# Weight sums made in memory around changes of operand, and a residual in row halves, in a split-fp32 decoder block

## The chip, the cores and the metric

One core of a Trainium2 chip runs one launch of the kernel. The metric is the device time in microseconds (us); a second execution is recorded by the hardware profiler. The core's engines work side by side, each in the order in which its instructions stand: TensorE (PE) multiplies, VectorE (DVE) and ScalarE (ACT) work on tiles, GpSimd (POOL) and SyncE (SP) here mostly issue DMAs. A DMA that an engine issues waits in that engine's order for what it needs, and everything behind it waits too.

## The reference

A decoder block in fp32 with 512 rows and width 2048. Two token mixers share one input projection, and the rest is a GeGLU channel mixer; the part that the change touches is the second half:

```
h    = rmsnorm(x) * g                     # x: 512 x 2048, after the mixers' residual
up   = h @ ffn_w_up                       # 2048 x 12288
up   = causal_dwconv(up, width 3)
gate, val = split(up)                     # 6144 columns each
x    = x + (gelu(gate) * val) @ ffn_w_down  # 6144 x 2048
out  = rmsnorm(x) * final_g
```

## The kernel before

**Precision.** Every fp32 operand is split in two: `h`, a rounded copy in fp32r (cast, ACT, L115), and `l`, the operand less `h` (DVE, L116). A product is three matmuls (`h·h`, `h·l`, `l·h`).

**Stages.** Input projection and mixers, the output projection (to about 561 us), the up product (to about 1575), the down product (to about 2052), and a tail with the last two pairs of rows of the down weights and the final norm.

**Products.** Up and down product use Strassen and Winograd's scheme: an operand tile of 2 x 2 quarters needs four sums of quarters, and seven block products take the place of eight. A tile is `q`, eight slots of 128 x 256: the quarters stand in slots 4 to 7, the four sums go to slots 0 to 3, and slots 0 to 6 are then split into a pair `wh`, `wl` (weights) or `ah`, `al` (activations). One **unit** is the seven products of one weight tile with one activation tile, 42 matmuls with 256 columns (`product`, L790), which add to seven PSUM banks. A **block** is the units that add to the same banks: 24 blocks of eight in the up product (gate and value by turns, two blocks to a group), and in the down product three chunks of 8, 8 and 6 activation tiles, each with four blocks, one to a column block of the output. At the end of an up block `combine` (L813) makes four quarters of the seven banks, and a convolution, a GELU and the multiplication follow as steps that are spread over the next block (`later`, L804); the results go to memory as `ad` (POOL, L869). At the end of a down block the banks are added to a residual tile `xs`, which POOL loads (L905) and writes back (L941).

**Weight sums.** For most weight tiles VectorE makes the sums: L590 (two of them at once, 128 x 512), L591 and L592. For 96 units, the last up block and all of the down product, L590's two sums are made beforehand in memory: POOL issues a copy and an accumulating DMA of 256 KB each (`make`, L681), one DMA to each up unit, and the load then takes the two sums (L584) and three quarters (L585).

**Order.** Weights and activations stand in one list, `stream`, each with `load`, `sums` and `pair`. `prepare` (L655) keeps the loads two places ahead of the pair, and the sums one. `ready(u)` says how far it must be before unit `u`'s products: two units' weights ahead, with the activations listed behind them. There are three `q` slots (pool `wq`), three pairs of weights, and one tile for each activation, which is free for the next chunk once its last product is through. An activation of the down product is listed after unit `s - 8 + spread[i] + 3`, where `s` is the chunk's first unit (L721 to L727). A **change of operand** is the stretch around `s` in which all activation tiles are replaced, one after the other; there are three (1: from up to down product, 2 and 3: between chunks). From the up product on each engine's order is as written in the program.

**The opening of the up product.** The first up block's activations come from the residual rows: four transposes (PE, L706) and an evacuation (ACT, L708) for each of two halves, sums (DVE, L615 to L617), and a pair. They are prepared one unit ahead of their product, beside that unit's weights. The residual rows are scaled first (`scale_rows`, on DVE at L696 and on ACT at L698).

Of the kernel before, what the change touches and what calls it, by code (L numbers as in the profile page):

```python
# [65 lines left out]

@with_exitstack
def hybrid_block(ctx: ExitStack, tc: tile.TileContext, x, xT, w_in, w_out, w_up, w_dn, w_us, w_ds, w_dl, wab, wsT, vec, bs, vgb, fg, out):
# [476 lines left out]

    x2[0] = load_x(0)
# [22 lines left out]

    def slots(name, n=8):  # L570
        return wq.tile([P, n, 256], F32, name=name, tag=name)

    class Weights:
# [5 lines left out]
        def load(self):  # L579
            self.q = q = slots("q")  # L580
            if self.made is None:
                nc.sync.dma_start(q[:, 4:8], self.src)
            else:
                nc.sync.dma_start(q[:, 2:4], self.made)  # L584
                nc.sync.dma_start(q[:, 4:7], self.src[:, 0:3])  # L585

        def sums(self):
            q = self.q
            if self.made is None:
                nc.vector.tensor_tensor(q[:, 2:4], q[:, 5:7], q[:, 7:8].broadcast_to([P, 2, 256]), ALU.add)  # L590
            nc.vector.tensor_tensor(q[:, 1], q[:, 2], q[:, 6], ALU.add)  # L591
            nc.vector.tensor_tensor(q[:, 0], q[:, 1], q[:, 4], ALU.add)  # L592
# [7 lines left out]
    class Acts:  # L600
# [18 lines left out]
        def pair(self):  # L619
# [3 lines left out]
            if self.fill is not None and self.m in (1, 3):  # L623
                scale_rows(2 + self.m // 2)
# [52 lines left out]
    sums_src = [w_us[m] for m in range(8)] + [w_ds[n, p] for c in CHUNKS for n in range(4) for p in c]  # L677
    for k, src in enumerate(sums_src):
        made[n_up - 8 + k] = tc.dram_tile([32, 2048], F32, name=f"made{k}")

    def make(u):  # L681

        k = u // 2
        if k < len(sums_src):
            how = {"accum_op": ALU.add, "max_dma_last_dim": 8192} if u % 2 else {"max_dma_last_dim": 8192}
            nc.gpsimd.dma_start(made[n_up - 8 + k], sums_src[k][u % 2], **how)  # L686
# [34 lines left out]
    spread = (0, 2, 3, 5, 7, 9, 10, 12)  # L721
# [16 lines left out]
    for u, (src, _) in enumerate(units):  # L738
        place[u] = len(stream)
        stream.append(Weights(src, made[u].rearrange("(p b) (c d e) -> (p b c) d e", p=32, c=4, d=2) if u in made else None))  # L740
# [34 lines left out]

    first = a_place[0]
# [7 lines left out]
    done[:] = [first + 2, first + 1, first + 1]  # L784
# [43 lines left out]
    def up_block(g, val, u0):  # L828
        q = {}
        for m in range(8):  # L830
# [5 lines left out]
            make(u0 + m)  # L836
# [56 lines left out]
    def down_block(ci, n, u0):  # L893
# [3 lines left out]
        for m in range(size):  # L897
            prepare(ready(u0 + m))
            if m == (6 if u0 == n_up else 1):
# [4 lines left out]
                xs[n] = pools["x"].tile([P, NS, 512], F32, name="xs", tag="xs", bufs=2)  # L904
                nc.gpsimd.dma_start(xs[n], x2d[n])  # L905
# [4 lines left out]
        X = xs[n]  # L910
        X11, X12, X21, X22 = X[:, 0:2, 0:256], X[:, 0:2, 256:512], X[:, 2:4, 0:256], X[:, 2:4, 256:512]
        c1, c6, c5, c7 = (pools["x"].tile([P, 2, 256], F32, name="cc", tag="cc", bufs=4) for _ in range(4))
        nc.scalar.copy(c1, q[1])  # L913
        tt(X11, X11, q[2], ALU.add)
        nc.scalar.copy(c6, q[6])
        nc.scalar.copy(c5, q[5])
# [4 lines left out]
            lambda: tt(X11, X11, c1, ALU.add),  # L921
            lambda: tt(c6, c6, c1, ALU.subtract),
# [14 lines left out]
        for i in range(4):  # L937
            later(at + i, steps[2 * i])
            later(at + i, steps[2 * i + 1])
        if ci < 2 or n < 2:  # L940
            later(at + 3, lambda: nc.gpsimd.dma_start(x2d[n], X))  # L941
# [6 lines left out]
    for n in range(2):  # L948
        xs[n] = slots("q").rearrange("p a b -> p (a b)").rearrange("p (a b) -> p a b", a=NS)
        nc.sync.dma_start(xs[n], x2d[n])  # L950
# [6 lines left out]
    for st in range(NS):  # L957
# [4 lines left out]
        for n, (i, d, lo, hi) in enumerate(pieces):  # L962
# [6 lines left out]
            t = xs[d][:, st, lo:hi]  # L969
            nc.vector.tensor_tensor(t, t, ps, ALU.add)  # L970
            sq = pools["x"].tile([P, 512], F32, name="sq", tag="cc", bufs=4)
# [16 lines left out]
        for n in order:  # L988
            _, d, lo, hi = pieces[n]
            t = xs[d][:, st, lo:hi]  # L990
# [70 lines left out]
```

## Time and profile before

| | us |
|---|---|
| median of three runs | 2107.61 (2106.12 to 2108.34) |
| profiled execution | 2107.67 |
| span of its instructions | 2106.0 |
| PE busy | 2048.9 (97%) |
| VectorE busy | 1746.8 (83%) |
| ScalarE busy | 911.5 (43%) |
| POOL busy | 185.9 (9%) |

The profiled execution's own time is the span and 1.67 us around it. The rows of slices show the span in 40 equal parts of 52.65 us, each digit the busy share in tenths. A row of windows has the length, then busy time and number of instructions of each engine, the granted clock of TensorE as a share of full speed, the mean busy share of the DMA engines, and GB/s. A row of groups has line, engine, operation, what is written from what, the shapes, the count, then busy us and mean ns of one, then idle time ahead of it and what ended most of it. A row of waits reads: engine and what waited, what it waited for, us in total, times, longest. Rows of DMA issues have KB each and the median us from issue to landing. Matmuls overlap, so PE's busy time counts no less than a stretch in which matmuls follow each other without a gap; a few matmul records are missing.

### The profile page before, as it was taken

How to read it: one execution, taken by the hardware profiler on the slowest of the kernel's cores; microseconds unless marked ns; L12 is line 12 of the kernel's file. 1: busy time of each engine (PE TensorE's matmuls, PEld its weight loads, DVE VectorE, ACT ScalarE, POOL GpSimd, SP SyncE). 2: the span in 40 equal slices, each digit the busy share in tenths (PEclk: the TensorE clock that was granted, in tenths of full speed). 3: DMA queues.
4: the chain of work that ended last, by engine and by line, in shares of the span. 5: the costliest groups of instructions: out<-in, count | busy, mean ns of one | idle time of the engine just before them, and what ended most of it. 6: DMA issues, size and time to landing. Idle time of an engine off the chain costs nothing.

```text
span 2106.0 us, 34882 instructions
## 1 busy us (share of the span) xinstructions
PE 2048.9 (97%) x14488; PEld 1928.0 (92%) x14488; DVE 1746.8 (83%) x2249; ACT 911.5 (43%) x899; POOL 185.9 (9%) x310
## 2 busy tenths in 40 slices
PE   9999999999889999999999999999988998999998
PEld 7888888888679999999999999999988998999996
DVE  7588972735379999999999999999989788778876
ACT  6445322413264444444444444444454344444443
POOL 1000000000010111111111112112110000000001
PEclk9999999999899999999999999999998999999999
DMA  8222322434133656556557557557565555645663
GB/s 276 89 84 95 102 100 100 160 104 166 70 103 118 175 152 185 163 161 188 155 166 195 161 156 200 152 156 198 164 190 175 206 177 193 233 163 202 231 235 120
DMA packets 91647, 338.08 MB, mean 161 GB/s; under 512 B 12768, under 2 KB 13408, under 8 KB 75616
## 3 DMA queue, kind: packets, MB, share of 16 engines
q1 hardware_dynamic: 71712, 236.60, 33.9%
q0 software_dynamic: 19200, 98.58, 17.0%
q8 instruction: 113, 1.85, 0.4%
q10 hardware_dynamic: 576, 0.66, 0.1%
q14 instruction: 46, 0.38, 0.1%
HBM read 304.34 MB, written 81.79 MB: 183 GB/s over the span
## 4 chain that ended last, share of the span: by engine, by line
PE 84%; DVE 10%; DMA 4%; issue 1%; ACT 1%; SPq 0%; DVEq 0%; ACTq 0%
PE qs L800 56%; PE ps L153 9%; PE ps L152 9%; PE ps L151 9%; DVE wl L116 3%; DVE al L116 2%; DMA q<-ad 1%; DMA q<-w_dn 1%; DMA q<-w_up 1%; DVE q L591 1%; DVE q L615 1%; PE qs L152 1%; PE qs L153 1%; PE qs L151 1%; DVE q L592 0%
## 5 line engine op out<-in xcount | busy, mean ns | idle before, releaser
L800 PE MATMUL qs<-al,wh 128*128 128x256 f32 x2688 | 763.8, 284 | 3.6 <-DVE al L116 3.5
L800 PE MATMUL qs<-ah,wh 128*128 128x256 f32 x2688 | 764.4, 284 | 2.7 <-DVE pad L817 1.8
L800 PE MATMUL qs<-ah,wl 128*128 128x256 f32 x2688 | 763.4, 284 | 2.8 <-DVE wl L116 2.8
L115 ACT CAST wh<-q 128x1792 fp32r<-128x1792 f32 (+1 forms) x282 | 476.7, 1691 | 651.1 <-PE qs L800 474.6
L116 DVE TENSOR_TENSOR wl<-q,wh 128x1792 fp32r<-128x1792 f32 (+1 forms) x282 | 567.9, 2014 | 55.4 <-ACT wh L115 55.1
L800 PEld LDWEIGHTS qs<-al,wh 128*128 128x128 f32 x2688 | 518.8, 193 | 4.5 <-DVE al L116 4.5
L800 PEld LDWEIGHTS qs<-ah,wh 128*128 128x128 f32 x2688 | 518.8, 193 | 3.2 <-DVE pad L817 2.0
L800 PEld LDWEIGHTS qs<-ah,wl 128*128 128x128 f32 x2688 | 518.7, 193 | 3.2 <-DVE wl L116 3.2
L800 PE MATMUL qs<-wh,ah 128*128 128x256 f32 x1232 | 353.7, 287 | 11.0 <-ACT cc L913 4.5
L800 PE MATMUL qs<-wl,ah 128*128 128x256 f32 x1232 | 353.7, 287 | 7.4 <-DVE wl L116 7.4
L800 PE MATMUL qs<-wh,al 128*128 128x256 f32 x1232 | 352.9, 286 | 3.9 <-DVE al L116 3.9
L800 PEld LDWEIGHTS qs<-wh,ah 128*128 128x128 f32 x1232 | 240.9, 196 | 12.2 <-ACT cc L913 4.9
L800 PEld LDWEIGHTS qs<-wl,ah 128*128 128x128 f32 x1232 | 240.9, 196 | 9.2 <-DVE wl L116 9.2
L800 PEld LDWEIGHTS qs<-wh,al 128*128 128x128 f32 x1232 | 240.8, 195 | 4.3 <-DVE al L116 4.3
L116 DVE TENSOR_TENSOR wl<-wraw,wh 128x1024 fp32r<-128x1024 f32 (+2 forms) x105 | 118.2, 1126 | 147.6 <-ACT wh L115 147.2
L115 ACT CAST wh<-wraw 128x1024 fp32r<-128x1024 f32 (+2 forms) x105 | 102.2, 975 | 272.2 <-PE ps L152 141.0
L151 PE MATMUL ps<-xgh,wh 128*128 128x512 f32 x384 | 152.5, 398 | 0.1
L152 PE MATMUL ps<-xgl,wh 128*128 128x512 f32 x384 | 152.2, 397 | 0.0
L153 PE MATMUL ps<-xgh,wl 128*128 128x512 f32 x384 | 150.5, 397 | 0.1
L591 DVE TENSOR_TENSOR q<-q 128x256 f32<-128x256 f32 x280 | 118.6, 424 | 29.7 <-DMA q<-w_dn 20.1
L686 POOL DMA_DIRECT2D made<-w_ds x176 | 115.3, 755 | 283.0 <-DMA made<-w_ds 273.8
L590 DVE TENSOR_TENSOR q<-q 128x512 f32<-128x512 f32 x184 | 126.1, 685 | 6.4 <-DMA q<-w_up 6.2
(244 smaller groups left out, 2418.5 us busy)
## 6 DMA issues: line engine op xcount, KB each, us to landing
q<-w_up SPq DMA_DIRECT2D x184, 512.0 KB, 3.6
made<-w_ds POOLq DMA_DIRECT2D x176, 256.0 KB, 4.4
q<-w_dn SPq DMA_DIRECT2D x88, 384.0 KB, 3.3
wraw<-w_in SPq DMA_DIRECT2D x28, 1024.0 KB, 4.8
q<-made SPq DMA_DIRECT2D x96, 256.0 KB, 2.6
wraw<-w_out SPq DMA_DIRECT2D x16, 1024.0 KB, 4.8
ad<-gate POOLq DMA_DIRECT2D x48, 256.0 KB, 2.4
q<-ad SPq DMA_DIRECT2D x24, 512.0 KB, 3.3
```

The lines of the kernel that those rows point to most:

```text
L115: nc.scalar.copy(h, src)
L116: nc.vector.tensor_tensor(l, src, h.bitcast(F32), ALU.subtract)
L151: nc.tensor.matmul(ps, lhsT=ah, rhs=bh, start=start, stop=False)
L152: nc.tensor.matmul(ps, lhsT=ah, rhs=bl, start=False, stop=False)
L153: nc.tensor.matmul(ps, lhsT=al, rhs=bh, start=False, stop=stop)
L590: nc.vector.tensor_tensor(q[:, 2:4], q[:, 5:7], q[:, 7:8].broadcast_to([P, 2, 256]), ALU.add)
L591: nc.vector.tensor_tensor(q[:, 1], q[:, 2], q[:, 6], ALU.add)
L615: nc.vector.tensor_tensor(q[:, 2:4], q[:, 7:8].broadcast_to([P, 2, 256]), q[:, 5:7], ALU.subtract)
L686: nc.gpsimd.dma_start(made[n_up - 8 + k], sums_src[k][u % 2], **how)
L800: nc.tensor.matmul(q[p][:, t], lhsT=x_, rhs=y_, start=first and t == 0 and n == 0, stop=last and t == 1 and n == 2, skip_group_check=True)
```

## The change

1. **Four sums instead of two, and other units.** `made_units` lists 46 units whose four sums are all made in memory: the first up block, and at each chunk the eight units before its first (in the down product only) and as many behind it as the chunk has activations. The last up block keeps two sums in memory. The other 50 down units have none: VectorE makes all four sums. A whole unit takes six DMAs on POOL (two copies and two accumulating ones of 256 KB, an accumulating one of 256 KB and one of 128 KB); the DMAs of neighbouring units are interleaved. The first up block's 48 stand on POOL behind the loads of the residual for the output projection; the other 244 are spread over the first 184 up units. A whole unit's load is 512 KB of sums and 384 KB of quarters.
2. **Activations earlier.** `spread` is (0, 1, 3, 4, 6, 7, 9, 10) instead of (0, 2, 3, 5, 7, 9, 10, 12).
3. **A fourth load buffer.** From the seventh unit of the down product on every fourth `q` comes from another pool.
4. **Residual in row halves.** Two tiles of 512 KB instead of one of 1024 KB, loaded in the second and the fourth unit of a block. The copy of the first bank on ACT goes; VectorE uses the bank itself, in five operations at the block's end and six spread behind it, instead of three and eight. Both halves are written back in every block but the last.
5. **Opening.** 40 matmuls whose result nobody uses ahead of the up product; the second activation is prepared ahead of the first unit; the ACT scalings of the residual stand one activation later.
6. **Tail.** Three column blocks instead of two are loaded again from memory for the tail.

```
+def made_units():
+    n_up = 24 * 8
+    starts = [n_up + 4 * (c[0] - CHUNKS[0][0]) for c in CHUNKS]
+    whole = list(range(8))
+    for c, s in zip(CHUNKS, starts):
+        whole += range(max(s - 8, n_up), s + len(c))
+    return whole, list(range(n_up - 8, n_up))
...
     def slots(name, n=8):
+        turn_of[0] += 1
+        if "x" in pools and turn_of[0] % 4 == 0:
+            return pools["x"].tile([P, n, 256], F32, name=name, tag=name)
         return wq.tile([P, n, 256], F32, name=name, tag=name)
...
-                nc.sync.dma_start(q[:, 2:4], self.made)
+                nc.sync.dma_start(q[:, 4 - self.made.shape[1]:4], self.made)
                 nc.sync.dma_start(q[:, 4:7], self.src[:, 0:3])
...
+            elif self.made.shape[1] == 4:
+                return
             nc.vector.tensor_tensor(q[:, 1], q[:, 2], q[:, 6], ALU.add)
...
-            if self.fill is not None and self.m in (1, 3):
-                scale_rows(2 + self.m // 2)
+            if self.fill is not None and self.m in (2, 4):
+                scale_rows(1 + self.m // 2)
...
+    order = sorted(rows)
+    to_make = in_turn(order[8:])
+    n_make = len(to_make)
+    make(start_make := in_turn(order[:8]), len(start_make))
...
-    spread = (0, 2, 3, 5, 7, 9, 10, 12)
+    spread = (0, 1, 3, 4, 6, 7, 9, 10)
...
+    idle = pools["tr"].tile([P, S], F32, name="tr", tag="tr")
+    for _ in range(40):
+        nc.tensor.matmul(idle[:, 0:256], lhsT=stream[0].hl[0][:, 0, 0:P], rhs=stream[0].hl[0][:, 1], start=True, stop=True)
...
-            make(u0 + m)
+            make(to_make, len(to_make) - n_make + n_make * (u0 + m + 1) // (n_up - 8))
...
-                xs[n] = pools["x"].tile([P, NS, 512], F32, name="xs", tag="xs", bufs=2)
-                nc.gpsimd.dma_start(xs[n], x2d[n])
+            for half, at in ((0, 6 if u0 == n_up else 1), (1, 6 if u0 == n_up else 3)):
+                if m == at:
+                    t = pools["x"].tile([P, 2, 512], F32, name="xs", tag="xs", bufs=3)
+                    nc.gpsimd.dma_start(t, x2d[n][:, 2 * half:2 * half + 2])
+                    xs[n, half] = t
...
-        nc.scalar.copy(c1, q[1])
+        tt(X11, X11, q[1], ALU.add)
         tt(X11, X11, q[2], ALU.add)
         nc.scalar.copy(c6, q[6])
+        tt(c6, c6, q[1], ALU.subtract)
...
-            lambda: tt(X11, X11, c1, ALU.add),
-            lambda: tt(c6, c6, c1, ALU.subtract),
```

**VectorE at the end of the last up block** (change 1). Line numbers of the changed kernel are higher: L126 is L116, L636 to L638 are L615 to L617, L872 is L817. Before; `wl_15158` is the first down unit's weights, `wl_15220` the second's:

```order
L615 TENSOR_TENSOR q_15106<-q_15106 128x512
L616 TENSOR_TENSOR q_15106<-q_15106 128x256
L617 TENSOR_TENSOR q_15106<-q_15106 128x256
L116 TENSOR_TENSOR wl_15158<-q_15051,wh_15157 128x1792
L591 TENSOR_TENSOR q_15161<-q_15161 128x256
L592 TENSOR_TENSOR q_15161<-q_15161 128x256
L116 TENSOR_TENSOR al3_15167<-q_15106,ah3_15166 128x1792
L591 TENSOR_TENSOR q_15170<-q_15170 128x256
L592 TENSOR_TENSOR q_15170<-q_15170 128x256
L116 TENSOR_TENSOR wl_15220<-q_15161,wh_15219 128x1792
L817 TENSOR_TENSOR pad0_4783<-c1_15268,qs_14807 128x2x256
```

Now; `wl_15251` and `wl_15303` are the same two units' weights:

```order
L126 TENSOR_TENSOR al3_15199<-q_15141,ah3_15198 128x1792
L919 SCALAR_TENSOR_TENSOR gate_15123<-pad0_4819,vc_73,gate_15123 128x512 x2
L126 TENSOR_TENSOR wl_15251<-q_15195,wh_15250 128x1792
L636 TENSOR_TENSOR q_15254<-q_15254 128x512
L637 TENSOR_TENSOR q_15254<-q_15254 128x256
L638 TENSOR_TENSOR q_15254<-q_15254 128x256
L126 TENSOR_TENSOR wl_15303<-q_15202,wh_15302 128x1792
L126 TENSOR_TENSOR al4_15310<-q_15254,ah4_15309 128x1792
L872 TENSOR_TENSOR pad0_4819<-c1_15357,qs_14901 128x2x256
```

The sums L591 and L592 of the weights are gone, and the fifth activation (`al4`) now stands ahead of the combine's first operation instead of the fourth.

**PE at the opening of the up product.** Before; `x2_2805` is the first 512 columns of the residual:

```order
L706 MATMUL tr_4183<-ident_88,x2_2805 128x128 x4
L706 MATMUL tr_4189<-ident_88,x2_2805 128x128 x4
L706 MATMUL tr_4207<-ident_88,x2_2805 128x128 x4
L706 MATMUL tr_4213<-ident_88,x2_2805 128x128 x4
L800 MATMUL qs_4219<-ah0_4202,wh_3987 128x256
```

Now (L754 is L706, L855 is L800):

```order
L827 MATMUL tr_4185<-wh_3992 128x256 x40
L754 MATMUL tr_4227<-ident_88,x2_2807 128x128 x4
L754 MATMUL tr_4233<-ident_88,x2_2807 128x128 x4
L754 MATMUL tr_4251<-ident_88,x2_2807 128x128 x4
L754 MATMUL tr_4257<-ident_88,x2_2807 128x128 x4
L754 MATMUL tr_4271<-ident_88,x2_3055 128x128 x4
L855 MATMUL qs_4277<-ah0_4246,wh_3992 128x256
```

The 40 matmuls, and a fifth group of transposes, for the third activation's first half, stand ahead of the first product.

**VectorE at the end of the last block of the first chunk** (change 2). Before:

```order
L116 TENSOR_TENSOR wl_17059<-q_17002,wh_17058 128x1792
L914 TENSOR_TENSOR xs_16723<-xs_16723,qs_16660 128x2x256
L917 TENSOR_TENSOR xs_16723<-xs_16723,qs_16681 128x2x256
L919 TENSOR_TENSOR xs_16723<-xs_16723,qs_16695 128x2x256
L615 TENSOR_TENSOR q_17062<-q_17062 128x512
```

Now (L972 to L979 are the block's end):

```order
L126 TENSOR_TENSOR wl_17114<-q_17017,wh_17113 128x1792
L126 TENSOR_TENSOR al4_17121<-q_17066,ah4_17120 128x1792
L972 TENSOR_TENSOR xs_16787<-xs_16787,qs_16719 128x2x256
L973 TENSOR_TENSOR xs_16787<-xs_16787,qs_16726 128x2x256
L975 TENSOR_TENSOR cc_17168<-cc_17168,qs_16719 128x512
L977 TENSOR_TENSOR xs_16787<-xs_16787,qs_16747 128x2x256
L979 TENSOR_TENSOR xs_16901<-xs_16901,qs_16761 128x2x256
```

Five operations instead of three stand at the block's end, and the fifth activation's pair ahead of them.

More of the change, by code (lines that the diff above doesn't have):

```diff
@@ L783, in hybrid_block @@
     rest_of_loads()
-    done[:] = [first + 2, first + 1, first + 1]
+    stream[first + 1].sums()
+    stream[first + 1].pair()
+    stream[first + 2].load()
+    done[:] = [first + 3, first + 2, first + 2]
     def qbank():
```

85 lines of the change are left out of this document (56 added, 29 removed).

## The prediction

> **What bounds the kernel now.** I read the slices first. Whole row PE (TensorE's matmuls) stands at 9 nearly everywhere; the dips are at slices 11 and 12 and in four places from slice 30 on, and in some of these the granted clock dips with it. VectorE is full between.
>
> ```profile
> PE   9999999999889999999999999999988998999998
> DVE  7588972735379999999999999999989788778876
> PEclk9999999999899999999999999999998999999999
> ```
>
> Then the windows, cut at these dips: PE busy time and records, then the other engines, clock, DMA share and GB/s.
>
> ```profile
> core 0: us, PE busy (x) PEld busy (x) DVE busy (x) ACT busy (x) POOL busy (x), PEclk, DMA share, GB/s
> 576.00:642.00 66.00, 53.76 (x395) 51.39 (x394) 51.42 (x62) 38.85 (x37) 6.56 (x12) 0.91 0.40 113
> 642.00:1550.00 908.00, 908.00 (x7556) 908.00 (x7556) 867.83 (x1100) 409.78 (x337) 137.86 (x217) 1.00 0.60 169
> 1550.00:1635.00 85.00, 72.22 (x535) 70.58 (x534) 76.25 (x92) 42.48 (x34) 4.05 (x7) 0.90 0.55 183
> 1740.00:1812.00 72.00, 62.94 (x497) 61.32 (x496) 60.82 (x73) 34.04 (x26) 1.59 (x3) 0.98 0.60 203
> 1920.00:1960.00 40.00, 36.82 (x290) 36.21 (x289) 36.18 (x45) 18.93 (x15) 0.54 (x1) 0.96 0.52 179
> ```
>
> The second row is the yardstick: 908.00/7556 = 0.1202 us per recorded matmul with PE never idle, so one unit (42 matmuls) is 5.05 us, and nothing can be won there. A disturbed stretch loses its length less its records times 0.1202. Change of operand 1 (1550 to 1635): 85 − 535 × 0.1202 = 20.7 us. Change 2 (1740 to 1812): 72 − 59.7 = 12.3. Change 3: 40 − 34.9 = 5.1. With the opening, treated below, this is all that the change can reach. What ends the waits there:
>
> ```profile
> DVE q L591 <- DMA q<-w_dn: 3.3, 4, 1.5
> DVE q L591 <- DMA q<-w_dn: 7.5, 4, 3.1
> DVE q L615 <- DMA q<-ad: 2.7, 2, 2.1
> PE qs L800 <- DVE wl L116: 4.8, 4, 1.9
> PE qs L800 <- DVE pad L817: 2.8, 1, 2.8
> PE qs L800 <- ACT c L816: 2.5, 1, 2.5
> ```
>
> The first is VectorE at change 1, the next two VectorE at change 2 (total us, times, longest), the last three PE at change 1. PE waits for VectorE, and VectorE partly for loads: it is the bound there, and a shorter queue on it shortens the stretch.
>
> **Prices.** Groups of instructions, busy us and mean ns of one:
>
> ```profile
> L116 DVE TENSOR_TENSOR wl<-q,wh 128x1792 fp32r<-128x1792 f32 x280 | 565.5, 2020 | 55.4 <-ACT wh L115 55.1
> L590 DVE TENSOR_TENSOR q<-q 128x512 f32<-128x512 f32 x184 | 126.1, 685 | 6.4 <-DMA q<-w_up 6.2
> L592 DVE TENSOR_TENSOR q<-q 128x256 f32<-128x256 f32 x280 | 119.0, 425 | 9.6
> L115 ACT CAST wh<-q 128x1792 fp32r<-128x1792 f32 x280 | 474.7, 1695 | 651.1 <-PE qs L800 474.6 <-DVE q L592 99.7 <-issue 28.4
> L864 DVE SCALAR_TENSOR_TENSOR gate<-pad,vc,gate 128x512 f32<-128x512 f32 x96 | 72.0, 749 | 1.7
> L867 DVE TENSOR_TENSOR gate<-gate,cv 128x512 f32<-128x512 f32 x48 | 33.2, 692 | 1.7
> L615 DVE TENSOR_TENSOR q<-q 128x512 f32<-128x512 f32 x30 | 20.6, 688 | 20.8 <-ACT q L708 14.2 <-DMA q<-ad 6.6
> L698 ACT ACTIVATE x<-x,rstd 128x512 f32<-128x512 f32 x8 | 5.1, 708 | 0.0
> L708 ACT ACTIVATE q<-tr,vc 128x512 f32<-128x512 f32 x16 | 11.0, 685 | 21.6 <-PE tr L706 20.8 <-DVE wl L116 0.8
> ```
>
> So on VectorE an activation tile, or a weight tile with all sums, is 0.69 + 0.43 + 0.43 + 2.02 = 3.56 us; a weight tile with two sums made in memory 2.87; with all four 2.02. The changed kernel has 46 of the last, 8 with two, and 50 down units that do all of it again (0.69 us more each). In the steady down blocks of 6 units such a unit needs 3.56 plus 13 block-end operations of 0.69 per six units (1.49), 5.05 of 5.05 us; the block of 8 has slack. That is hidden, just.
>
> **Opening, −9.1.** The stretch from PE's first product to the end of its last wait there, by the products (L800) and by the transposes (L706) alone, two waits in it, and the clock:
>
> ```profile
> 576.39:641.47 65.08, 48.52 (x342) 45.84 (x342) 0.91 0.40 114
> 576.39:641.47 65.08, 7.93 (x48) 5.65 (x48) 0.91 0.40 114
> PE tr L706 <- ACT q L708: 5.9, 5, 1.9
> PE qs L800 <- DVE al L116: 3.5, 3, 1.7
> 564.00:569.00 5.00, 1.66 (x4) 0.73 (x4) 3.33 (x15) 0.69 (x1) 0.00 (x0) 0.55 0.51 210
> 576.00:581.00 5.00, 4.86 (x23) 4.61 (x22) 1.88 (x4) 0.69 (x1) 0.00 (x0) 0.50 0.31 105
> ```
>
> What will still be there: 342 products at 0.1202 are 41.1; a group of four transposes takes 7.93/12 = 0.66, and of twelve groups one moves ahead of the first product, 7.3; the half clock costs half of 5 us, 2.4; the four ACT scalings of a residual tile (L698, 4 × 0.71 = 2.8), which stand ahead of an evacuation twice, show by my estimate 1.6 each time, 3.2; the wait at the block's end for the combine 2.0. Sum 56.0, so 65.1 − 56.0 = 9.1 goes: a unit here needs 2.02 + 3.56 = 5.6 us of VectorE instead of 2.02 + 1.54 + 3.56 = 7.1, against 5.05 + 2 × 0.66 = 6.4 of PE, so VectorE falls behind PE and the chain through it opens. Bounds: −4, if the ACT chain (two evacuations 0.69, two casts 1.70: 4.8 of 6.4 us, each behind PE) goes on costing the 5.9 of the first wait; −12, the sum of the waits with the scalings hidden.
>
> The 40 idle matmuls are 4.8 us from about 561.6, when out_proj ends and PE waits for the rows anyway: cost nothing. The row 564 to 569 has the clock down about 3 us after the last product, and the first product comes 10 us later than the idle ones end, so it starts at half clock as before: gain 0, and 2.4 if the clock did stay up.
>
> **Change 1, −6.0.** Before, VectorE's work from eight units ahead to the eighth activation: 13 weight tiles × 2.87 = 37.3, 8 activations × 3.56 = 28.5, two gate rests 3.0 (two of 0.75 to a rest), the combine 7 × 0.69 = 4.85, four value rests 8.8 (two of 0.75 and 0.69 each): 82.4 us against 13.5 units of PE, 68.4: 14.0 over, and waits for loads 5.3 (3.3 + 1.2 + 0.8): 19.3 of the 20.7 measured. After: five tiles 2.87, eight 2.02: 75.7, 7.3 over, and the loads' waits go with the fourth slot. But the order matters: ahead of the combine (L872) VectorE now has five activations instead of four, 5 × 2.87 + 2 × 2.02 + 5 × 3.56 + 6.0 (four gate rests) = 42.2 us against 7 × 2.87 + 4 × 3.56 + 6.0 = 40.3, so PE's waits at the boundary (2.8 + 2.5 and about 2.3 for the activation) stay and grow by 1.9: 9.5. The clock falls to half behind it once more, 2.2 to 2.5, and the tile backlog at the end of the next block, which reaches its five residual operations 3.9 us late where 1.5 is free, adds 2.5. Left 14.5, gain 6. Bounds −2 (the backlog repeated) and −13 (only the 7.3 stay). I take the middle by the order, the nearest thing to a row.
>
> **Changes 2 and 3, −11.0 and −4.6.** Change 2 before: 37.3 + 28.5 + 14 block-end operations 9.7 = 75.5, and the last tile's cast 1.7: 77.2, against some 15 units of PE, 75.2: 2.0 over, and 10.2 of waits for loads (7.5 + 2.7), 12.2 of the 12.3. After: eleven tiles with four sums 22.2 + 28.5 + 15 operations 10.3 + 1.7 = 62.7, and up to 5.5 of a tile begun before: 68.2, with 7 in hand, and the loads come a unit earlier with the fourth slot. I leave 1.3, since VectorE's queue up to the pair of the sixth unit, counted the same way, ends within 0.7 us of its product. Bounds −7 and −12.3. Change 3 goes the same way by 4.6 of 5.1 (−3 to −5.1).
>
> **The rest.** The last block's boundary +1.2 (0 to +2): last_a's two pairs (1.22 each) and an extra 0.69 stand ahead of the five operations. The tail −1.3 (0 to −1.4): two operations moved ahead of PE's last wait. The 244 POOL DMAs instead of 192 lie beside the up product, which they can slow only through its loads; median landings, in the order 645 to 695, 720 to 745, then whole run, then start-up:
>
> ```profile
> q<-w_up SPq DMA_DIRECT2D x10, 512.0 KB, 3.6
> q<-w_up SPq DMA_DIRECT2D x5, 512.0 KB, 4.4
> q<-w_dl SPq DMA_DIRECT2D x4, 1024.0 KB, 4.8
> xs<-x2d POOLq DMA_DIRECT2D x12, 1024.0 KB, 6.8
> wraw<-w_in SPq DMA_DIRECT2D x15, 256.0 KB, 7.0
> 422.80 0.75 POOL L524 DMA_DIRECT2D x<-x  x1 [13.65 <-issue]
> 472.40 1.51 SPq L582 DMA_DIRECT2D q<-w_up  x3
> ```
>
> A w_up load issued one unit and a half ahead may take about 6.4 us before its tile is late (1.5 × 5.05 = 7.6 from slot to need, less 0.69 + 0.43); 3.6 quiet and 4.4 in a POOL burst leave room, so 0 (0 to +6, for a few late ones). The first 48 DMAs start behind the last x load at 423.6; the first three sums are wanted by SP at 472.4, where 18 DMAs at 2.5 us (ten in the 25 us window) are done by 469: hidden, but close.
>
> Sum: −9.1 − 6.0 − 11.0 − 4.6 + 1.2 − 1.3 = −30.8. The profiled execution took 2107.67 (span 2106.0 and 1.67 around it), 0.06 over the median of the runs, so 2107.67 − 30.8 = **2076.9**, told as 2077. For the likeliest alone the bounds give 2069 to 2087 (its terms do not fail together).
>
> **Rivals.** A, the loads of the whole units are late (chance 0.15). A unit now loads 512 + 384 = 896 KB, whose landing the rows of 1024 KB bound by 4.8 and 6.8 us; at the upper one the three changes give only half, 21.6/2 = 10.8 back: 2088. Against it: eight loads in a row, not a steady need, and the fourth slot. B, change 1 vanishes too, because the combine is not delayed (0.08): 2077 − 13 = 2064. C, slower (0.06): the made DMAs come in bursts, because POOL first stands at the value rows (L869) and then catches up with 1.33 a unit instead of 1. Before, such a burst makes the w_up load 4.4 us instead of 3.6; above 6.4 it decides. At 7.0, the start-up row, each of eight units in each of eleven pairs is 0.6 late: 8 × 11 × 0.6 = 53, with −30.8: 2129. Against it: twice the step of 0.8 gives only 5.2.
> The Trainium skill ("DMA: Bandwidth & Descriptors", Queues, rings and completion order) says that each DMA engine turns between the queues that have work, packet by packet; by that rule a second queue that is always busy costs the load up to its own time again, as an estimate 7.2 us, and 88 units late by 0.8 make 70, 2147; the trace, 4.4 with both queues busy, doesn't show it so far.
> D, the plan isn't what it seems: a sum isn't ready when its load is issued, SP stands, and the gain is eaten (0.04): 2100 to 2108.
>
> **Chances.** Forecast 0.67, A 0.15, B 0.08, C 0.06, D 0.04. Two runs of this kernel can be told apart from about 0.2% (4.2 us). Faster: 0.67 + 0.15 + 0.08 and a third of D, 0.91; I lower it to 0.90 for several small misses together; same 0.03; slower 0.07. The range goes from 2066 (between B and the forecast's own edge) to 2094 (beyond A, with 0.1 above it).
>
> **What would show it.** Right: the windows of changes 2 and 3 at 0.1202 us a matmul with under 2 us lost; change 1 still with a stop of some 9 us at the combine and the clock at half behind it; the first up block about 9 us shorter, its first products still at half clock; w_up landings under 6 us, and the steady part without waits. Wrong: waits for q<-made on VectorE or ACT at the changes (A), no boundary stop (B), DVE waits at L590's successor in the up product (C), SP standing at made2 (D). The forecast falls if plain units of 5.05 us no longer hide on VectorE: then each of the 50 costs what it is late.

## The result, and the profile after

The changed kernel takes 2091.95 us (median), against 2106.86 for the kernel before in the same comparison; the ratio is 0.9918, with a 95% interval of 0.9903 to 0.9932. The forecast was 2077 with a range of 2066 to 2094: the sign and the range hold, but only about half of the 30.8 us came (14.9 by the medians, 17.3 by the ratio). The runs spread more than before, 2083.1 to 2094.8 against 2104.1 to 2109.9. One more run of the changed kernel took 3297.64 us at a mean granted clock of 0.556; it is left out of the ratio and of this spread but not of the median, which is 2091.32 without it. The profiled execution took 2092.59 us, with a span of 2090.9: 15.1 less than before's.

The windows of the changed kernel, at the same stretches; the first is cut at 1535, ahead of its change 1, and one up to 2040 is added, which holds the last block's end:

```profile
core 0: us, PE busy (x) PEld busy (x) DVE busy (x) ACT busy (x) POOL busy (x), PEclk, DMA share, GB/s
642.00:1535.00 893.00, 882.02 (x7292) 877.69 (x7291) 836.86 (x1058) 397.13 (x325) 184.74 (x264) 1.00 0.66 175
1550.00:1635.00 85.00, 76.12 (x600) 74.43 (x599) 80.40 (x89) 45.30 (x36) 3.31 (x6) 0.96 0.61 209
1740.00:1812.00 72.00, 71.05 (x590) 70.64 (x589) 66.12 (x73) 34.92 (x25) 3.17 (x6) 1.00 0.70 237
1920.00:1960.00 40.00, 40.00 (x336) 40.00 (x335) 38.28 (x47) 16.92 (x12) 3.17 (x6) 1.00 0.68 222
1960.00:2040.00 80.00, 78.85 (x650) 78.35 (x649) 70.40 (x86) 34.54 (x30) 6.63 (x13) 1.00 0.64 204
```

With the yardstick of the prediction (0.1202 us a recorded matmul; missing records make each loss uncertain by some tenths, and by about 2 us in the long first window, where PE's idle time alone is 11.0 us) the stretches lose, in us:

| stretch | before | after | difference | forecast |
|---|---|---|---|---|
| steady up product | −0.2 | 893 − 7292 × 0.1202 = 16.5 | +16.7 | 0 |
| change 1 | 20.7 | 85 − 72.1 = 12.9 | −7.8 | −6.0 |
| change 2 | 12.3 | 72 − 70.9 = 1.1 | −11.2 | −11.0 |
| change 3 | 5.1 | 40 − 40.4 = −0.4 | −5.5 | −4.6 |
| last block's boundary | −0.5 | 80 − 78.1 = 1.9 | +2.4 | +1.2 |

At change 1 PE still stops where the last up block ends:

```profile
PE qs L855 <- ACT c L871: 4.0, 1, 4.0
PE qs L855 <- DVE wl L126: 1.9, 3, 1.2
...
PE qs L855 <- DVE pad L872: 1.2, 1, 1.2
```

The opening is best read from the products (L800 before, L855 after) that are through at 645 us. The windows of these lines alone, before and after:

```profile
560.00:645.00 85.00, 52.62 (x364) 49.71 (x365) 0.85 0.35 106
```

```profile
560.00:645.00 85.00, 57.57 (x441) 55.06 (x442) 0.96 0.49 145
```

441 − 364 = 77 products more, 9.3 us; forecast −9.1. The output projection, which the change does not touch, ends at the same time in the two, at 562.8 us (the last L520 before, L530 after). All of these together make −14.7, of the 15.1 by which the span is shorter. So the opening and the three changes each gave about the forecast amount, and the steady up product, where nothing can be won, took 16.7 us back.

The waits in that window show who is late. VectorE before, then VectorE and PE after:

```profile
DVE q L590 <- DMA q<-w_up: 3.6, 8, 1.1
```

```profile
DVE q L609 <- DMA q<-w_up: 29.8, 23, 4.4
DVE q L612 <- DMA q<-w_up: 1.7, 1, 1.7
```

```profile
PE qs L855 <- DVE pad L872: 6.8, 7, 2.3
PE qs L855 <- DVE v L878: 2.9, 10, 0.3
PE qs L855 <- DVE wl L126: 1.1, 2, 0.7
```

VectorE waits 29.8 us for weight loads of the up product instead of 3.6. It then comes late to the combine at the block's end (L872 to L878), and PE waits there for its PSUM banks. Two neighbouring stretches of the changed kernel, and the DMA issues of the same two, in the same order:

```profile
902.40:939.60 37.20, 37.20 (x311) 37.16 (x311) 36.19 (x47) 16.61 (x14) 3.13 (x6) 1.00 0.38 131
939.60:976.80 37.20, 35.24 (x292) 34.86 (x291) 33.24 (x44) 14.59 (x12) 12.68 (x19) 1.00 0.86 215
```

```profile
q<-w_up SPq DMA_DIRECT2D x7, 512.0 KB, 3.6
made<-w_m POOLq DMA_DIRECT2D x4, 256.0 KB, 5.5
...
made<-w_m POOLq DMA_DIRECT2D x14, 256.0 KB, 6.3
q<-w_up SPq DMA_DIRECT2D x7, 512.0 KB, 6.2
```

Where POOL issues 19 DMAs in 37 us, the DMA engines are busy 0.86 of the time, a w_up load lands after 6.2 us in the median instead of 3.6, and PE stands for 2 us; where it issues 6, nothing is lost. The second of these stretches in the kernel before had 13 POOL instructions, a DMA share of 0.69, a median landing of 3.7 us and no loss:

```profile
939.60:976.80 37.20, 37.20 (x313) 37.20 (x312) 36.19 (x46) 17.11 (x13) 8.30 (x13) 1.00 0.69 188
```

A burst and its loss do not always go together. Over 1014.0 to 1051.2 POOL issued 20 DMAs, the DMA share was 0.84, the loads landed after 5.2 us in the median, and PE stood for 0.02 us. The largest loss, 3.7 us over 1162.8 to 1200.0, stands where POOL had 8 instructions: a burst over 1110 to 1150, with a median landing of 6.1 us, had made VectorE wait 4.4 us for one load, PE stood at the next block's end, and behind that stop the granted clock was 0.66 for 5 us, which is 1.3 of the 3.7.

POOL is quiet in between because it stands at the writes of the gated activations, as its waits over 642 to 1550 show:

```profile
POOL ad L924 <- DVE gate L922: 549.8, 43, 67.5
POOL made L728 <- DMA made<-w_m: 140.2, 65, 6.9
```

### The profile page after: what moved, and what is told of

It reads as the page before. It is cut to its first block, busy times and chain, and to the rows that moved or that the text cites. A ratio compares the mean times of both kernels' runs of the same rounds, so it can differ in the third digit from the quotient of the medians.

```text
span 2090.9 us, 34973 instructions
## 1 busy us (share of the span) xinstructions
PE 2045.2 (98%) x14528; PEld 1923.7 (92%) x14528; DVE 1738.6 (83%) x2199; ACT 906.7 (43%) x887; POOL 283.2 (14%) x434
## 3 DMA queue, kind: packets, MB, share of 16 engines
q0 software_dynamic: 36288, 119.83, 24.3%
## 4 chain that ended last, share of the span: by engine, by line
PE 71%; DVE 20%; DMA 5%; issue 2%; ACT 1%; SPq 0%; DVEq 0%; ACTq 0%
PE qs L855 42%; PE ps L161 9%; PE ps L163 9%; PE ps L162 9%; DVE wl L126 8%; DMA q<-w_up 4%; DVE q L609 2%; DVE al L126 1%; DVE q L612 1%; DMA q<-ad 1%; DVE cv L919 1%; DVE gate L919 1%; PE qs L162 1%; PE qs L161 1%; PE qs L163 1%
## 5 line engine op out<-in xcount | busy, mean ns | idle before, releaser
L855 PE MATMUL qs<-ah,wh 128*128 128x256 f32 x2688 | 765.3, 285 | 12.3 <-DVE pad L872 8.6
L855 PE MATMUL qs<-ah,wl 128*128 128x256 f32 x2688 | 762.1, 284 | 2.8 <-DVE wl L126 2.8
L855 PE MATMUL qs<-al,wh 128*128 128x256 f32 x2688 | 761.8, 283 | 2.1 <-DVE al L126 2.1
L126 DVE TENSOR_TENSOR wl<-q,wh 128x1792 fp32r<-128x1792 f32 (+1 forms) x282 | 567.7, 2013 | 47.8 <-ACT wh L125 47.6
L855 PEld LDWEIGHTS qs<-ah,wh 128*128 128x128 f32 x2688 | 517.0, 192 | 16.7 <-DVE pad L872 10.5
L855 PEld LDWEIGHTS qs<-ah,wl 128*128 128x128 f32 x2688 | 516.9, 192 | 3.6 <-DVE wl L126 3.6
L855 PEld LDWEIGHTS qs<-al,wh 128*128 128x128 f32 x2688 | 517.0, 192 | 2.3 <-DVE al L126 2.3
L855 PE MATMUL qs<-wh,ah 128*128 128x256 f32 x1232 | 350.5, 285 | 8.5 <-ACT c L871 4.0
L855 PE MATMUL qs<-wl,ah 128*128 128x256 f32 x1232 | 350.0, 284 | 0.8 <-DVE wl L126 0.6
L855 PE MATMUL qs<-wh,al 128*128 128x256 f32 x1232 | 349.7, 284 | 0.0
L855 PEld LDWEIGHTS qs<-wh,ah 128*128 128x128 f32 x1232 | 237.6, 193 | 9.8 <-ACT c L871 4.2
L728 POOL DMA_DIRECT2D made<-w_m x292 | 209.9, 863 | 268.6 <-DMA made<-w_m 255.5
L855 PEld LDWEIGHTS qs<-wl,ah 128*128 128x128 f32 x1232 | 237.6, 193 | 1.4 <-DVE wl L126 1.4
L855 PEld LDWEIGHTS qs<-wh,al 128*128 128x128 f32 x1232 | 237.6, 193 | 0.0
L126 DVE TENSOR_TENSOR wl<-wraw,wh 128x1024 fp32r<-128x1024 f32 (+2 forms) x105 | 118.0, 1125 | 143.5 <-ACT wh L125 143.2
L609 DVE TENSOR_TENSOR q<-q 128x512 f32<-128x512 f32 x226 | 154.9, 685 | 31.5 <-DMA q<-w_up 29.8
L924 POOL DMA_DIRECT2D ad<-gate x48 | 28.1, 585 | 668.0 <-DVE gate L922 631.9
```

Of the source, the lines that this page charges most:

```text
L126: nc.vector.tensor_tensor(l, src, h.bitcast(F32), ALU.subtract)
L728: nc.gpsimd.dma_start(dst, src, max_dma_last_dim=8192, **how)
L855: nc.tensor.matmul(q[p][:, t], lhsT=x_, rhs=y_, start=first and t == 0 and n == 0, stop=last and t == 1 and n == 2, skip_group_check=True)
L924: nc.gpsimd.dma_start(ad[2 * g + n][:, at:at + 2], gate.rearrange("p (a b) -> p a b", a=2))
```

## The experiments

### Is it the made DMAs, and is it their bursts?

**Paced.** The theory: the made DMAs are not too many but come too densely, since POOL is held for up to 67 us and then issues what has piled up. The edit puts one small POOL copy ahead of each unit's DMAs:

```
+    pace = const.tile([P, 1], F32, name="pace")
...
+            if to_make:
+                nc.gpsimd.tensor_copy(pace, stream[place[u0 + m]].hl[0][:, 0, 0:1])
             make(to_make, len(to_make) - n_make + n_make * (u0 + m + 1) // (n_up - 8))
```

> Changed kernel, with one small POOL copy ahead of each up unit's made DMAs; it reads the unit's weights, so POOL can issue the 1.33 DMAs of a unit no earlier than that unit's weights are cast. The same DMAs, without the bursts that follow each value block. Burst theory (dense made DMAs delay the w_up loads, which costs the 16.6 us of the steady up product, 642 to 1535): loss there under 5 us, total about 2080. Load theory (the 27% more POOL traffic costs the same however it is spread): loss 14 to 20 us, total 2089 to 2096. If the w_up loads aren't the cause at all: as the changed kernel, 2092.

Measured: 2071.36 us, ratio to the kernel before 0.9827 (0.9813 to 0.9842). The steady up product and the waits of VectorE and of POOL in it:

```profile
642.00:1535.00 893.00, 891.50 (x7420) 890.52 (x7419) 852.16 (x1079) 402.15 (x331) 295.46 (x445) 1.00 0.69 181
```

```profile
DVE wl L126 <- ACT wh L125: 11.1, 13, 1.5
DVE q L609 <- DMA q<-w_up: 5.2, 6, 1.9
```

```profile
POOL ad L927 <- DVE gate L925: 271.8, 43, 13.7
POOL pace L893 <- ACT wh L125: 267.1, 82, 5.6
```

It loses 893 − 7420 × 0.1202 = 1.1 us instead of 16.5, with the same 292 DMAs and a DMA share that is even a little higher (0.69 against 0.66). POOL's longest wait at the writes falls from 67.5 to 13.7 us. The load theory falls: it is the bursts that cost, not the traffic.

Not all of the 20 us by which the kernel is faster than the changed one is spacing. The output projection, ahead of everything that the edit is about, ends 2.7 us sooner. Its last step on VectorE, in the changed kernel and in the paced one:

```profile
560.04 2.79 DVE L530 SCALAR_TENSOR_TENSOR x<-ps,rstd_g,x 128x512 f32<-128x512 f32 x4 [11.97 <-PE ps L163]
```

```profile
557.33 2.79 DVE L530 SCALAR_TENSOR_TENSOR x<-ps,rstd_g,x 128x512 f32<-128x512 f32 x4 [11.97 <-PE ps L163]
```

This goes with the pace: the step ends at 562.8 to 563.7 us in the five kernels without it, and at 559.7 to 560.7 in eight of the nine with it (the three-slot kernel is the ninth, at 563.3; it had 61 matmuls in its first 20 us, the paced one 75). Why one more constant tile does this is open. Kernels with and without the pace are therefore compared from the end of that step on.

**No made DMAs.**

```
+    unmade = {}
+    for k, u in enumerate(whole):
+        unmade[u] = w_m4[k, 0:512].rearrange("(p a) c -> p a c", p=P)
...
+    rows = {u: [] for u in rows}
...
-        stream.append(Weights(src, made.get(u)))
+        stream.append(Weights(src, unmade.get(u)))
```

> Changed kernel without any made DMA: the loads take rows of the host's lists as they are in place of the sums, so the sums of the 54 units are left out of the computation; everything else is the same, the loads' sizes too. Either theory on traffic: the steady up product loses under 1 us, and the wait for w_up near 609 us goes, total 2070 to 2076. If the made DMAs aren't the cause: the loss stays at some 16 us, 2090.

Measured: 2071.02 us (0.9825, 0.9810 to 0.9839), the same as the paced kernel. It has no pace, though, and its output projection ended 3.2 us later; from there on its profiled execution takes 1506.2 us, against the paced kernel's 1508.7 and the changed one's 1528.1. So with the pace, making the sums still costs about 2.5 us, and without it some 22. The up product runs without a gap:

```profile
642.00:1535.00 893.00, 893.00 (x7445) 893.00 (x7443) 854.41 (x1084) 404.48 (x333) 23.79 (x44) 1.00 0.37 120
```

**Fewer made DMAs, of either kind.** POOL's queue went from 19200 to 36288 packets, much more than its bytes (98.58 to 119.83 MB), so small packets were a rival. The two edits drop two of each whole unit's DMAs:

```
+    rows = {u: r[:2] for u, r in rows.items()}
```

```
+    rows = {u: r[:1] + r[2:] if len(r) > 2 else r for u, r in rows.items()}
```

> Changed kernel without the last two accumulating DMAs of each whole unit (256 KB in rows of 2 KB and 128 KB in rows of 1 KB; two of its four sums lack a summand): 200 made DMAs, all of 256 KB, about as many as the 192 before. Theory of small packets (POOL's queue went from 19200 to 36288 packets): loss in the steady up product under 2 us, total about 2077. Theory of bursts by count: 14 instead of 21 DMAs to a pair of blocks, loss 2 to 6 us, about 2080.

> Changed kernel without the two accumulating DMAs of 256 KB in long rows of each whole unit (its four sums lack a summand): 200 made DMAs as in the run without the small ones, but with the small-packet ones kept. Theory of small packets: loss in the steady up product stays at 10 us or more, total 2086 to 2092. Theory of bursts by count: 2 to 6 us, about 2080, as in that run.

Measured: 2076.48 us without the small ones (0.9845, 0.9825 to 0.9866), and 2070.91 without the big ones (0.9826, 0.9812 to 0.9841). The windows of the two, in this order:

```profile
642.00:1535.00 893.00, 890.24 (x7402) 888.55 (x7401) 849.70 (x1078) 403.32 (x331) 125.11 (x196) 1.00 0.57 163
```

```profile
642.00:1535.00 893.00, 892.99 (x7442) 892.82 (x7442) 853.81 (x1081) 405.43 (x332) 128.50 (x196) 1.00 0.57 158
```

Both are without a pace, and both lose little (3.3 us and, by the count of records, nothing) at 200 DMAs. Small packets are not the cause: the kernel that keeps them is the better one. Fewer DMAs in a burst is enough, as in the kernel before with its 192. Why the kernel with long rows alone loses 3 us more isn't settled, and one of its four runs, 2070.41, was as fast as the other kernel. It issues two copies and right behind them the two accumulating DMAs that wait for these, where the other has a DMA of the unit before in between; this was not tried alone.

### What carries the changes of operand

All further runs start from the paced kernel (2071.36), since its steady part no longer hides a difference.

**Three slots.**

```
-        if "x" in pools and turn_of[0] % 4 == 0:
+        if False:
```

> Paced kernel without the fourth load slot. Prediction (the slot takes the waits for loads at the changes, which were 10.2 us at change 2 and some 4 us each at 1 and 3): 5 to 14 us slower, 2076 to 2085. Rival (with the four sums made VectorE is far enough ahead to hide the loads without it): within 2 us, 2070 to 2073.

**Two sums instead of four around changes 2 and 3.**

```
-        whole += range(max(s - 8, n_up), s + len(c))
-    return whole, list(range(n_up - 8, n_up))
+        whole += range(s, s + len(c)) if s == n_up else []
+    halved = list(range(n_up - 8, n_up))
+    for c, s in zip(CHUNKS[1:], starts[1:]):
+        halved += range(s - 8, s + len(c))
+    return whole, halved
```

> Paced kernel with two sums in memory instead of four for the units around changes 2 and 3 (172 made DMAs instead of 292). Theory of the prediction (at change 2 VectorE's work was 2.0 us over and the waits for loads 10.2, which the fourth slot takes): 2 to 5 us lost at each of the two, total 2075 to 2080. Rival (the fourth slot alone carries both changes): 2069 to 2072.

Measured: 2093.61 us with three slots (0.9929, 0.9913 to 0.9944), and 2077.99 with two sums (0.9859, 0.9844 to 0.9874). The first is 22 us over the paced kernel, more than the 5 to 14 that were expected. The windows of changes 2 and 3, of the paced kernel, of the one with three slots and of the one with two sums:

```profile
1720.00:1800.00 80.00, 80.00 (x669) 80.00 (x668) 75.29 (x86) 38.32 (x27) 4.22 (x8) 1.00 0.70 237
1895.00:1950.00 55.00, 55.00 (x459) 54.82 (x458) 51.96 (x65) 21.87 (x16) 4.22 (x8) 1.00 0.70 221
```

```profile
1720.00:1800.00 80.00, 72.24 (x583) 71.23 (x582) 67.13 (x72) 37.22 (x27) 3.16 (x6) 0.98 0.68 223
1895.00:1950.00 55.00, 49.30 (x388) 48.89 (x387) 45.07 (x49) 25.08 (x20) 2.11 (x4) 0.94 0.66 229
```

```profile
1720.00:1800.00 80.00, 75.94 (x615) 75.17 (x614) 78.41 (x98) 37.02 (x26) 4.24 (x8) 0.98 0.62 200
1895.00:1950.00 55.00, 51.95 (x431) 51.54 (x430) 53.86 (x69) 24.81 (x19) 3.85 (x8) 1.00 0.61 194
```

The paced kernel loses nothing at either. With three slots the two lose 80 − 583 × 0.1202 = 9.9 and 8.4 us, while VectorE is busy only 67 of 80 us, and its waits at change 2 are for loads:

```profile
DVE q L636 <- DMA q<-ad: 9.0, 4, 3.2
DVE q L609 <- DMA q<-w_dn: 2.9, 1, 2.9
```

With two sums they lose 6.1 and 3.2 us, VectorE is busy 78.4 of 80 us, and it waits 0.5 us for loads. So there are two limits, one behind the other: the loads, which the fourth slot takes away, and VectorE's work, which the sums take away. Either of the two alone leaves half of the loss or more: at change 2 it was 12.3 with neither (the kernel before, which also has the old spread and the old residual), 9.9 with the sums, 6.1 with the slot, and −0.4 with both. At change 3 the sums without the slot cost more than both missing did (8.4 against 5.1); a weight tile's load is 896 KB there instead of 640, which may hold the slots for longer, but this was not tried alone.

**The old spread at change 1.**

```
+            wide = (0, 2, 3, 5, 7, 9, 10, 12) if s == n_up else spread
-            after.setdefault(s - 8 + spread[i] + 3, []).append(Acts(i, src=ad[p]))
+            after.setdefault(s - 8 + wide[i] + 3, []).append(Acts(i, src=ad[p]))
```

> Paced kernel, with the old spread (0, 2, 3, 5, 7, 9, 10, 12) at change 1 alone. Theory of the prediction (the stop at the boundary is the fifth activation, 3.56 us of VectorE, ahead of the combine): the stop of 6.1 us at the combine shrinks by about 3.6 us, total 2067 to 2069 against 2071.4. Rival (VectorE's total work sets the end of change 1, 7.3 us over): what the boundary gains is lost at the later activations, 2070 to 2073, or more.

Measured: 2071.17 us (0.9820, 0.9803 to 0.9836), the same as paced. PE's waits at change 1 in the paced kernel, and with the old spread:

```profile
PE qs L856 <- ACT c L872: 3.9, 1, 3.9
PE qs L856 <- DVE xs L976: 1.4, 1, 1.4
PE qs L856 <- DVE wl L126: 0.7, 1, 0.7
PE qs L856 <- DVE pad L873: 0.6, 1, 0.6
```

```profile
PE qs L857 <- DVE al L126: 2.8, 1, 2.8
PE qs L857 <- DVE pad L874: 1.2, 1, 1.2
PE qs L857 <- ACT c L873: 1.1, 1, 1.1
```

The stop at the combine falls from 4.5 us (3.9 and 0.6) to 2.3, as the theory has it, and 2.8 us of waiting for an activation comes in its place. The order says where PE stops. By the window, change 1 loses 80 − 585 × 0.1202 = 9.7 us with the old spread, against 10.4.

**The last up block's sums in memory too,** with the new spread and with the old one:

```
-        whole += range(max(s - 8, n_up), s + len(c))
-    return whole, list(range(n_up - 8, n_up))
+        whole += range(s - 8, s + len(c))
+    return whole, []
```

> Paced kernel, with all four sums of the last up block made in memory too (324 made DMAs instead of 292, 1.5 to a unit instead of 1.33). Theory (VectorE's total work sets the end of change 1, which loses 10.4 us in the paced kernel): 8 x 0.85 = 6.8 us less work there, so a loss of 4 to 7 us, total 2065 to 2068. Rival (the paced made DMAs are close to what the w_up loads bear): the steady up product loses 3 to 8 us, total 2071 to 2077.

> The kernel of the run before with the old spread at change 1. Theory (with VectorE's work cut, the order ahead of the combine counts): another 2 to 4 us less, 2062 to 2066. Rival (as with the old spread alone, what the stop gains comes back later): within 1 us of the run before.

Measured: 2067.21 us (0.9809, 0.9793 to 0.9825) and 2065.88 us (0.9806, 0.9787 to 0.9824). Both are below the paced kernel by 4 to 5.5 us, with intervals that overlap its own a little; between the two there is no difference that the times alone can tell. Change 1 of the first, then the steady up product and change 1 of the second:

```profile
1535.00:1615.00 80.00, 73.75 (x585) 72.32 (x584) 74.38 (x81) 41.89 (x34) 3.29 (x6) 0.96 0.65 221
```

```profile
642.00:1535.00 893.00, 893.00 (x7444) 893.00 (x7443) 851.35 (x1072) 405.22 (x334) 316.01 (x474) 1.00 0.74 191
1535.00:1615.00 80.00, 75.55 (x609) 74.56 (x608) 76.66 (x85) 43.06 (x34) 3.31 (x6) 0.98 0.64 217
```

Even 324 DMAs, at a DMA share of 0.74, cost the up product nothing when they are paced, so the rival of the load falls a second time. Change 1 loses 80 − 609 × 0.1202 = 6.8 us with the old spread, but 80 − 585 × 0.1202 = 9.7 with the new one, where 4 to 7 were expected. So less work on VectorE alone wins 0.7 us there, as the old spread alone did, and both together win 3.6: PE's stop at the combine is 4.5 us in the paced kernel, 2.3 with the old spread, 4.0 with less work, and 0.3 with both. What the first of these kernels gains in time is thus not at change 1; the windows put 2.6 us of it into the steady up product (7442 products against 7420), which is near the uncertainty of that window. The second is the fastest kernel of the study, some 25 us below the changed one.

### What carries the opening

Three edits undo one part each, on the paced kernel: the idle matmuls are taken out; the first block's sums go back to VectorE; the order of the second activation and of the scalings goes back.

```
-    idle = pools["tr"].tile([P, S], F32, name="tr", tag="tr")
-    for _ in range(40):
-        nc.tensor.matmul(idle[:, 0:256], ...)
```

```
-    whole = list(range(8))
+    whole = []
...
-    to_make = in_turn(order[8:])
+    to_make = in_turn(order)
-    make(start_make := in_turn(order[:8]), len(start_make))
```

```
-            if self.fill is not None and self.m in (2, 4):
-                scale_rows(1 + self.m // 2)
+            if self.fill is not None and self.m in (1, 3):
+                scale_rows(2 + self.m // 2)
...
-    stream[first + 1].sums()
-    stream[first + 1].pair()
-    stream[first + 2].load()
-    done[:] = [first + 3, first + 2, first + 2]
+    done[:] = [first + 2, first + 1, first + 1]
```

> Paced kernel without the 40 idle matmuls. Prediction (they end 10 us ahead of the first product, and the transposes are hidden by VectorE): no difference, 2070.5 to 2072.3. Rival (they hold the clock for the transposes and let the opening's chain of transposes and evacuations run sooner): 1 to 3 us slower, 2072.5 to 2074.5.

> Paced kernel with the first up block's weight sums made on VectorE again (48 made DMAs less). Prediction (VectorE's 1.54 us a unit there are what the opening gained): 8 to 12 us slower, 2079 to 2083. Rival (the gain came from the order of the first two activations and the scalings): 0 to 4 us slower, up to 2075.

> Paced kernel with the opening's old order: the second activation prepared beside the first unit, and the ACT scalings of the residual one activation earlier; made sums and idle matmuls stay. Theory (of the 77 products by which the changed kernel is ahead at 645 us, the made sums and the idle matmuls carry a part, and the order the rest, some 5.9 us): 3 to 7 us slower than paced, 2074 to 2078. Rival (the order carries nothing, the sums and the clock all): within 1.5 us of paced, 2070 to 2073.

The products are counted over 82.17 us from the end of the output projection (562.79 us before, 560.12 paced), so that its earlier end does not count as a gain of the opening. Only these products, in the paced kernel:

```profile
560.12:642.29 82.17, 59.13 (x439) 56.70 (x440) 0.92 0.51 149
```

| kernel | us | over paced | products in 82.17 us |
|---|---|---|---|
| paced | 2071.36 | | 439 |
| without idle matmuls | 2075.24 | 3.9 | 423 |
| first block's sums on VectorE | 2074.66 | 3.3 | 411 |
| old order | 2075.31 | 4.0 | 410 |
| before | 2108.82 | | 364 |

The ratios to the kernel before are 0.9844 (0.9829 to 0.9858), 0.9838 (0.9823 to 0.9852) and 0.9845 (0.9829 to 0.9862), each beside paced's 0.9827 (0.9813 to 0.9842); the intervals overlap, so the count of products is the better evidence. Six more kernels with the paced one's opening, the changed one among them, have 436 to 446 in the same stretch. The opening's gain in the paced kernel is 75 products, 9.0 us; undoing the idle matmuls takes back 16 (1.9 us), the sums 28 (3.4) and the order 29 (3.5). Together that is 8.8 us: the three add up. With the old order the first product even comes 1.9 us sooner after the output projection (12.3 us instead of 14.2), and yet fewer are through at the end. In the kernel without idle matmuls the rest of the 3.9 us is not at the opening; it loses 2.5 us more than the paced one around change 1 (1535 to 1720), and why is open.

What the idle matmuls do, in the kernel without them and in the paced one:

```profile
564.00:569.00 5.00, 3.32 (x11) 1.99 (x12) 1.82 (x5) 1.37 (x2) 0.00 (x0) 0.50 0.05 20
```

```profile
564.00:569.00 5.00, 2.74 (x17) 1.64 (x15) 2.36 (x6) 1.37 (x2) 0.00 (x0) 0.91 0.00 0
```

With them the first three of the five groups of transposes ahead of the first product take 0.82, 0.66 and 0.71 us; without them 1.66, 1.11 and 1.11. The last two take 1.11 to 1.12 us in both. The chain of waits shows the length of the first group of four, in the kernel without them and in the paced one:

```profile
564.13 1.68 PE tr L754 x4
```

```profile
564.61 0.83 PE tr L754 x4
```

These transposes stand on the chain: over 560 to 576 us they are 31.6% of it in the kernel without idle matmuls.

## Why the prediction was right and wrong

**The range held by luck in part.** 2092 lies above the bounds that the prediction gave for its forecast alone (2069 to 2087). The range reached to 2094 because of rival A, at 2088, and A did not occur.

**The opening, −9.1: the size was right (−9.3), the reason about a third of it.** The step that failed is that the gain is VectorE's 1.54 us a unit, and that the idle matmuls gain nothing. The sums alone are worth 3.4 us by the count of products, the idle matmuls 1.9 and the order 3.5. The prediction looked only at whether the clock is up at the first product, and there it was right; it asked nothing about the transposes ahead of it, which stand on the chain and ran at half clock. That three causes add up to the size forecast for one is luck.

**Change 1, −6.0: measured −7.8.** The stop at the combine stayed, as forecast, but it was 5.2 us in the changed kernel (4.0 for the copy of the first bank and 1.2 for the combine) where the sum has 9.5. The granted clock fell behind it again, to 0.67 and 0.65 over the two windows of 5 us from 1585. Neither bound was the right one alone: with the old spread the stop shrinks and the loss hardly moves (9.7 instead of 10.4), with less work on VectorE the loss hardly moves either (9.7), and only both together bring it to 6.8. So the middle between the order's bound and the total's was luck in part.

**Changes 2 and 3, −11.0 and −4.6: measured −11.2 and −5.5.** The split at change 2, 2.0 us of work and 10.2 of loads, holds in kind (15 units are 75.7 us and not 75.2, so the work was 1.5 over; the forecast does not hang on it): the loads need the slot and the work needs the sums. It is not a sum of two independent parts, though; without the slot 9.9 us are lost again, without the second pair of sums 6.1. Rival A (late loads of 896 KB) did not occur with the fourth slot; without it the two changes lose 18.3 us, more than A's 10.8.

**The last boundary and the tail.** +1.2 was +2.4 by the window, and no gain of the tail is seen in what is left of the span; both are small.

**The steady up product, 0 (0 to +6): measured +16.7. This is the step that failed,** and with it half of the gain went. The mechanism was there as rival C, with the place (the bursts behind the value rows), the releaser (L869), the threshold of 6.4 us and the sign to look for (waits of VectorE at L590's successor, which came: 29.8 us at L609), but at a chance of 0.06 and as a case that would make the kernel slower in all. The error is a size: from 3.6 quiet and 4.4 in a burst the text went to 5.2 by a second step of 0.8. But a burst is now longer as well as denser, 19 POOL instructions in 37 us against 13 in the same stretch before, and the landing there was 6.2 us in the median. Put into C's own formula, a landing of 6.2 would still cost nothing, because it is under 6.4; but it is a median, and the 23 waits, of up to 4.4 us, are for single loads that came late. C's cost is neither nothing nor 53 us; it belonged into the sum as a term, not among the rivals. The Trainium skill's rule ("DMA: Bandwidth & Descriptors", Queues, rings and completion order: each DMA engine turns between the queues that have work) gave 7.2 as an estimate for a second queue that is always busy, and the measured 6.2 lies halfway between it and the 5.2 that stood against it. The whole run's median landing of w_up, 3.6 before and 4.1 after, would not have shown it either: the kernel with 324 paced DMAs has 4.2 and loses nothing.

**What the paced kernel says of the rest.** Without that term the forecast 2077 stands against 2071.4 measured. In the profiled executions 2.7 us of this are the earlier end of the output projection, which no term is about. The opening came as forecast (9.0 us); change 1 gave more, 20.7 − 10.4 = 10.3 us instead of 6.0, and changes 2 and 3 a little more, since nothing is left there.

## What to carry to other kernels

When work is moved from a compute engine to DMAs that "lie beside" it, price them by the landing times in the densest stretch, not by a median or a mean share over the whole run, and look at what holds their issuing engine: a queue that stands at a wait and then catches up makes bursts. A cheap instruction on the issuing engine that reads something of each step spaces the DMAs out; here it brought 15 us back in the stretch that had lost them. Before two profiles are compared at a fixed time, look whether the stages ahead of it ended at the same time in both. And where a stretch has two limits close together (loads and work), removing either alone buys less than its share, so test them by undoing one at a time from the kernel that has both.

## What was not expected of the hardware

- The same 292 DMAs of a second queue (244 of them behind the up product), at nearly the same mean DMA share (0.66 and 0.69), cost 16.5 us in bursts and 1.1 us when spaced; a 512 KB load took 3.6 us in the median in a quiet stretch and 6.2 us in a dense one.
- Five us of otherwise useless matmuls kept the granted clock up over the first three groups of transposes behind them, where it was 0.50 without, and the first group of four took 0.83 instead of 1.68 us; that was worth 1.9 us of the opening.
